# Two norms in one pass ahead of a convolution, its modulation later, and a feed-forward that begins with one token tile

## The chip, the cores and the metric

The kernel runs on one core of one Trainium2 chip. The metric is the time of one execution in microseconds on the device: the median of 3 runs is 2066.24 us (2065.29 to 2067.12). The engines are named as in the profile: PE is TensorE (matmuls; PEld are its weight loads), DVE is VectorE, ACT is ScalarE, POOL is GpSimd, SP is SyncE.

## What is computed

Two models run one after the other on 256 tokens of width 1024. The first is an attention layer with a large expert layer behind it. The second has two layers over the 256 tokens of its input ("latent") and 256 tokens of context; each layer is a mixer (first a short convolution, then a latent attention) and a feed-forward, and each of these begins with a norm whose output is scaled and shifted ("modulated") by rows computed from a conditioning vector `c`. What the change touches, cut from the reference:

```python
x = first_block(...)                  # ends with: return rmsnorm(h, final_norm_g)
silu_c = silu(c)
for i in range(2):
    sh1, sc1, g1, sh2, sc2, g2 = split(silu_c @ mod_w[i] + mod_b[i], 6)      # also from c_ctx, for the context
    a_lat = modulate(rms_norm(h_lat, norm_mix_g[i]), sh1, sc1)               # h * (1 + scale) + shift
    o_lat = short_conv_mixer(a_lat, ...) if i == 0 else mla_mixer(a_lat, ...)
    h_lat = h_lat + g1 * o_lat
    h_lat = h_lat + g2 * swiglu(modulate(rms_norm(h_lat, norm_ffn_g[i]), sh2, sc2), ...)
return h_lat
```

So the end of the first model is a norm over each token's 1024 values with the gain `final_norm_g`, and the beginning of the second is another norm over the result.

## The kernel before

**Matmuls.** Each product of two f32 matrices is made of three matmuls in a rounded f32 form: high part of the weight by high part of the activation, high by low, low by high. In `s_mode` these are lines 278 (`whi` by the high half of `act`), 279 (`whi` by the low half) and 280 (`wlo` by the high half). A piece of 128x128 of the weight is the stationary operand, and is loaded anew for each matmul; the activations stream past it, 512 columns where latent and context go together, 256 where only the 256 latent tokens do. In `m_mode` (lines 312, 313, 315) the weights stream.

**Weights.** `Stream W` loads weight tiles of 128x1024 in the order of a plan: SP issues the DMA into one of 4 `raw` buffers, ACT rounds it into `whi` (line 108), DVE subtracts to get `wlo` (line 109); there are 3 pairs of `whi` and `wlo`. A tile has a number in its name (`wlo474`). `W.prime(n)` brings the splits forward.

**Norm and modulation of an activation.** `norm_rows` squares and sums a token tile of 128x1024 on ACT, makes the mean on DVE (line 415, 128x1), raises it to -1/2 on POOL (`pow`, line 416) and multiplies on DVE. At the end of the first model it writes `hk = hk*yns*gate` (line 428, `gate` being the gain `fg`, which a POOL DMA of line 1161 spreads over the partitions); then `modulated` calls it again for the second norm (`yn`, line 426). `modulated` transposes `yn` on PE (line 1129), scales and shifts on ACT (line 1134, into `trs`), and splits into the two halves of `act` on DVE (the cast of line 1136, the subtraction of line 1137).

**The start of a mixer or feed-forward** works in pieces: `s_mode` takes `lead=(slices, function)`; its first three weight tiles go over the columns of the first slice, then the function makes the activations of the second slice, and the same three tiles go over it. For the convolution `BOTH` is used: first the 256 context tokens, then the 256 latent ones. The second feed-forward, `ffn(1, (0,), ...)`, has latent tokens alone, so it has no `lead`: each of its weight tiles is 24 matmuls of 256 columns.

**The modulation rows of the convolution** are made beside its matmuls. `second(M)` is a generator of background work, advanced by `run(..., bg, 1.7)` at each weight tile: `modulation(0, b)` for b=1 and b=2. It loads pieces of `mod_w` (`mraw`) with POOL's DMAs (line 488), multiplies and sums most of them on DVE (lines 504 and 506, into `ms`), the rest on PE (line 524), folds the sums on PE (line 529), adds the bias on DVE (line 531, `mb`), sends the result to DRAM and back with POOL's DMAs (`moddr<-mb`, line 534, then `mr<-moddr`, line 535), and transposes what comes back on PE (line 540). The first feed-forward has the same generator in it for the next layer, with buffers that are called `mem` there.

**Order.** Outside `tc.manual_schedule` blocks a scheduler orders the instructions of each engine by its own estimates; inside them, and for instructions with `tc.keep_in_program_order`, the order of the code holds. Each engine then works strictly in its order.

Of the kernel before, what the change touches and what calls it, by code (L numbers as in the profile page):

```python
# [19 lines left out]
P = 128  # L20
D = 1024
# [135 lines left out]
def tile_kernel(ctx: ExitStack, tc: tile.TileContext, I, out, cst, dbg=None):  # L157
# [320 lines left out]
    def modulation(i, b, raw, ahead, acc, room, sel, cc=None):  # L478
# [16 lines left out]
        loads = [load(n) for n in range(ahead)]  # L495
        sums = [acc(w) for w in ws]
        for n in range(2 * own):
            k, h = divmod(n, 2)
            r = loads.pop(0)
            hs = slice(h * D, (h + 1) * D)  # L500
            for w in ws:
                o, c = sums[w][:, hs], silu_c[:, w, k:k + 1]
                if k == 0:
                    V.tensor_scalar(o, r, c, None, op0=ALU.mult)
                else:
                    V.scalar_tensor_tensor(o, r, c, o, op0=ALU.mult, op1=ALU.add)  # L506
            if n + ahead < 2 * KC:
                loads.append(load(n + ahead))
            yield
# [255 lines left out]
    with ExitStack() as pp:  # L765
# [353 lines left out]

        def modulated(i, s, w, act, N_, xn=None, trs=2):  # L1120

            ah, al = act
            xn = xn or normed(w, N_)
            cs = slice(w * T, (w + 1) * T)
            for k0 in range(0, KC, 2):
                ps = misc()
                for k in range(2):
                    for t in range(2):
                        TE.transpose(ps[:, k * T + t * P:k * T + (t + 1) * P],
                                     xn[t][:, (k0 + k) * P:(k0 + k + 1) * P], ident)  # L1130
                a = N_.tile([P, 2, T], F32, tag="trs", name=uid("trs"), bufs=trs)
                for k in range(2):
                    o = w * 48 + 24 * s + k0 + k
                    S.activation(a[:, k, :], ps[:, k * T:(k + 1) * T], AF.Identity,
                                 scale=scl[i][:, 2 * w + s, k0 + k:k0 + k + 1], bias=modc[i][:, o:o + 1])
                V.tensor_copy(ah[:, k0:k0 + 2, cs], a)  # L1136
                V.tensor_tensor(al[:, k0:k0 + 2, cs], a, ah[:, k0:k0 + 2, cs].bitcast(F32), op=ALU.subtract)  # L1137

# [29 lines left out]
    for t in range(2):  # L1168
        for h in range(2):
            hs = slice(h * 512, (h + 1) * 512)  # L1170
            V.tensor_tensor(hx[t][:, hs], hx[t][:, hs], ov[t][h], op=ALU.add)
        norm_rows(BP, hx[t], "yn", fg, into=hx[t])
        dump(f"x1_{t}", hx[t])

# [12 lines left out]
    def ffn(i, ws, then, xn):  # L1187
# [6 lines left out]
        else:  # L1194
            modulated(i, 1, ws[0], act, BP, xn)
        ah, al = (x[:, :, :N] for x in act)
# [56 lines left out]
    with tc.tile_pool(name="conv", bufs=1) as C, tc.tile_pool(name="mod", bufs=1) as M:  # L1253
        bg = second(M)
        bt = res.tile([P, 2, KC, 2 * T], F32R, tag="x1", name="bt")
        bh, bl = bt[:, 0], bt[:, 1]
# [23 lines left out]
        for f in range(2):  # L1280
            run(s_mode(8, 512, ah, al, 2 * T, e_c,
                       lead=None if f else (BOTH, lambda: modulated(0, 0, 0, act, BP))), bg, 1.7)
            run(s_mode(8, 512, ah, al, 2 * T, lambda n, ps: e_u(n, ps, f)), bg, 1.7)
            run(s_mode(8, 512, ah, al, 2 * T, lambda n, ps: e_b(n, ps, f)), bg, 1.7)
        drain(bg)
# [37 lines left out]
    with ExitStack() as pm:  # L1323
# [208 lines left out]
        with tc.manual_schedule(engines={V.engine, S.engine, G.engine}):  # L1532
            run(m_mode(8, 1024, oh, ol, (0, 1), e_out))
            xn.append(finish(1))

    ffn(1, (0,), lambda t, h: nc.sync.dma_start(out[t * P:(t + 1) * P, h:h + 512], hx[t][:, h:h + 512]), xn)


# [25 lines left out]
```

## Time and profile before

| | before |
|---|---|
| median of 3 runs | 2066.24 us |
| profiled execution, its time | 2068.81 us |
| its span | 2067.0 us |
| PE busy | 2001.2 us, 97% |
| DVE busy | 1436.4 us, 69% |
| ACT busy | 904.7 us, 44% |
| POOL busy | 429.7 us, 21% |

The span is that of the instructions of one execution; its time has 1.8 us more around it. PE is busy for nearly the whole span, so time is won by taking away one of PE's few waits or some of its matmuls, and lost by adding to either. Rows of the timeline give the start, the duration, the engine, the line, the output and inputs, the shape, how many instructions a row gathers, and in brackets the idle time of the engine ahead of it with what ended it.

### The profile page before, as it was taken

The page shows a single profiled execution, that of the slowest core. Times are in us where ns is not written, and L with a number is a line of the kernel's source. Part 1 is how long each engine was busy: PE and PEld are TensorE (multiplying, and loading weights), DVE is VectorE, ACT ScalarE, POOL GpSimd, SP SyncE. Part 2 cuts the span into 40 slices and gives each one's busy share as a digit, 9 for nine tenths or more (in the row PEclk, how much of TensorE's full clock was granted, in tenths as well). Part 3 has the DMA queues.
Part 4 walks back from the last instruction along what each step waited for, and adds up shares of the span by engine and source line. Part 5 has one row for each costly group of instructions (what it writes and reads, how often), then busy time and mean ns, then how long its engine had stood idle before and what let it go on. Part 6 is the DMA issues. An engine that isn't in the chain of part 4 may idle for free.

```text
span 2067.0 us, 33205 instructions
## 1 busy us (share of the span) xinstructions
PE 2001.2 (97%) x12513; PEld 1743.1 (84%) x12513; DVE 1436.4 (69%) x2664; ACT 904.7 (44%) x1537; POOL 429.7 (21%) x394
## 2 busy tenths in 40 slices
PE   8999999999999999999999998999999989899999
PEld 7899899999999888888778777877888878568997
DVE  4666699978888888889577758656432477756554
ACT  4565544443444444445453223322322367555443
POOL 0002556655555100010021212021000034200000
PEclk9999999999999999999999999999999999999999
DMA  7445666665555544487565745466422345125654
GB/s 223 138 122 185 173 182 177 185 169 146 161 154 154 194 155 161 155 283 259 188 223 180 262 131 189 142 217 228 139 92 92 125 141 158 42 71 153 184 184 143
DMA packets 187172, 344.15 MB, mean 166 GB/s; under 512 B 18412, under 2 KB 95876, under 8 KB 187012
## 3 DMA queue, kind: packets, MB, share of 16 engines
q1 hardware_dynamic: 166036, 279.62, 43.9%
q0 software_dynamic: 17440, 59.14, 8.9%
q10 hardware_dynamic: 3536, 3.28, 0.6%
q8 instruction: 98, 1.61, 0.3%
q14 instruction: 62, 0.51, 0.1%
HBM read 339.78 MB, written 2.18 MB: 165 GB/s over the span
## 4 chain that ended last, share of the span: by engine, by line
PE 84%; issue 6%; DVE 5%; DMA 3%; ACT 1%; POOL 1%; POOLq 0%; DVEq 0%; ACTq 0%
PE acc L278 9%; PE acc L279 9%; PE acc L280 9%; PE acc L247 6%; PE acc L248 6%; PE acc L249 6%; PE acc L1070 5%; PE acc L1071 5%; PE acc L1074 5%; PE acc L312 5%; PE acc L313 5%; PE acc L315 5%; PE misc L1043 3%; DMA mem<-in_mod_w_dram 1%; PE misc L1468 1%
## 5 line engine op out<-in xcount | busy, mean ns | idle before, releaser
L109 DVE TENSOR_TENSOR wlo<-raw,whi 128x1024 fp32r<-128x1024 f32 (+2 forms) x401 | 484.0, 1210 | 399.9 <-ACT whi L108 398.7
L108 ACT ACTIVATE whi<-raw 128x1024 fp32r<-128x1024 f32 (+1 forms) x412 | 430.0, 1046 | 667.9 <-PE acc L279 271.4
L278 PE MATMUL acc<-act,whi 128*128 128x512 f32 (+1 forms) x944 | 323.1, 344 | 2.0 <-DVE act L1136 2.0
L280 PE MATMUL acc<-act,wlo 128*128 128x512 f32 (+1 forms) x944 | 322.1, 342 | 2.5 <-DVE wlo L109 2.5
L279 PE MATMUL acc<-act,whi 128*128 128x512 f32 (+1 forms) x944 | 322.9, 342 | 1.7 <-DVE act L1137 1.7
L247 PE MATMUL acc<-x2h,uhi 128*128 128x256 f32 x1024 | 293.7, 287 | 0.0
L248 PE MATMUL acc<-x2l,uhi 128*128 128x256 f32 x1024 | 290.6, 284 | 0.0
L249 PE MATMUL acc<-x2h,ulo 128*128 128x256 f32 x1024 | 290.6, 284 | 0.0
L791 POOL TENSOR_TENSOR ulo<-ut,uhi 128x768 fp32r<-128x768 f32 x128 | 238.0, 1861 | 173.8 <-ACT uhi L789 138.9
L789 ACT ACTIVATE uhi<-ut 128x768 fp32r<-128x768 f32 x128 | 108.6, 848 | 222.8 <-PE acc L248 90.8
L278 PEld LDWEIGHTS acc<-act,whi 128*128 128x128 f32 x944 | 180.9, 193 | 29.1 <-ACT whi L108 3.4
L1070 PE MATMUL acc<-whi,g 128*128 128x512 f32 x512 | 202.7, 396 | 0.2 <-ACT g L108 0.2
L280 PEld LDWEIGHTS acc<-act,wlo 128*128 128x128 f32 x944 | 181.3, 192 | 22.7 <-DVE wlo L109 2.9
L1071 PE MATMUL acc<-wlo,g 128*128 128x512 f32 x512 | 199.9, 390 | 0.3 <-DVE wlo L109 0.3
L279 PEld LDWEIGHTS acc<-act,whi 128*128 128x128 f32 x944 | 181.5, 192 | 21.9 <-DVE act L1137 2.5
L247 PEld LDWEIGHTS acc<-x2h,uhi 128*128 128x128 f32 x1024 | 197.9, 193 | 0.0
L248 PEld LDWEIGHTS acc<-x2l,uhi 128*128 128x128 f32 x1024 | 197.4, 193 | 0.0
L249 PEld LDWEIGHTS acc<-x2h,ulo 128*128 128x128 f32 x1024 | 197.3, 193 | 0.0
L1074 PE MATMUL acc<-whi,g 128*128 128x512 f32 x512 | 158.0, 390 | 0.0
L777 DVE STREAM_TRANSPOSE ut<-raw 128x768 f32<-128x768 f32 x128 | 123.4, 964 | 0.0
L506 DVE SCALAR_TENSOR_TENSOR mem<-mem,silu_c 128x1024 f32<-128x1024 f32 x84 | 106.7, 1284 | 17.2 <-DMA mem<-in_mod_w_dram 16.9
L1074 PEld LDWEIGHTS acc<-whi,g 128*128 128x128 f32 x512 | 96.0, 188 | 21.0 <-DVE g L109 0.5
(396 smaller groups left out, 3708.8 us busy)
## 6 DMA issues: line engine op xcount, KB each, us to landing
raw<-in_peer_u_dram SPq DMA_DIRECT2D x512, 128.0 KB, 3.2
raw<-in_peer_v_dram SPq DMA_DIRECT2D x128, 512.0 KB, 3.4
mem<-in_mod_w_dram POOLq DMA_DIRECT2D x64, 512.0 KB, 5.1
raw<-in_ffn_w_down_dram SPq DMA_DIRECT2D x50, 512.0 KB, 3.3
raw<-in_ffn_w_gate_dram SPq DMA_DIRECT2D x44, 512.0 KB, 3.8
raw<-in_ffn_w_up_dram SPq DMA_DIRECT2D x44, 512.0 KB, 3.7
raw<-in_w_in_dram SPq DMA_DIRECT2D x40, 512.0 KB, 3.9
mraw<-in_mod_w_dram POOLq DMA_DIRECT2D x32, 512.0 KB, 5.0
```

The source lines that it names most:

```text
L108: a = self.nc.scalar.activation(hi, src, AF.Copy)
L109: b = (eng or self.nc.vector).tensor_tensor(lo, src, hi.bitcast(F32), op=ALU.subtract)
L247: mm(ps, lh, rh, start=first, stop=False)
L248: mm(ps, lh, rl, start=False, stop=False)
L249: mm(ps, ll, rh, start=False, stop=last)
L278: mm(ps[n][:, cs], hi[:, k - k0, c], xh[:, k, cs], start=first, stop=False)
L279: mm(ps[n][:, cs], hi[:, k - k0, c], xl[:, k, cs], start=False, stop=False)
L280: mm(ps[n][:, cs], lo[:, k - k0, c], xh[:, k, cs], start=False, stop=last)
L791: a = eng.tensor_tensor(lo[:, c], x, hi[:, c].bitcast(F32), op=ALU.subtract)
L1070: mm(ov[t][h], gh[:, ts], vh[:, 0, hs], start=j == 0, stop=False)
L1071: mm(ov[t][h], gh[:, ts], vl[:, 0, hs], start=False, stop=False)
L1074: mm(ov[t][h], gl[:, ts], vh[:, 0, hs], start=False, stop=j == P - 1)
```

## The change

It has three parts. First, the two norms at the border of the models are made in one pass: ACT squares `hk`, DVE multiplies `hk` by the gain at once (without waiting for the first mean), ACT squares the product, and the two factors are combined in 128x1 columns of `cols`, so that `yn` is one multiplication of the product by the combined factor. `scaled()` multiplies `hk` by its own factor later. Second, the background generator of the convolution stops after its loads are issued, runs no step during the first `s_mode`, and then goes on at 1.95 steps a weight tile. Third, the second feed-forward begins with one token tile of 128 columns, then the other, and two of its weight tiles are split ahead of its norm's activations.

```diff
@@ modulation
         loads = [load(n) for n in range(ahead)]
         sums = [acc(w) for w in ws]
+        if cc is not None and b == 1:
+            yield
         for n in range(2 * own):
...
                 if k == 0:
-                    V.tensor_scalar(o, r, c, None, op0=ALU.mult)
+                    a = V.tensor_scalar(o, r, c, None, op0=ALU.mult)
+                    if cc is not None and b == 1:
+                        tc.keep_in_program_order(a)
@@ modulated
-        def modulated(i, s, w, act, N_, xn=None, trs=2):
+        def modulated(i, s, w, act, N_, xn=None, trs=2, one=None):
...
-            cs = slice(w * T, (w + 1) * T)
-            for k0 in range(0, KC, 2):
+            tiles = range(2) if one is None else [one]
+            n = P * len(tiles)
+            per = 2 * T // n
+            cs = slice(w * T + tiles[0] * P, w * T + tiles[0] * P + n)
+            for k0 in range(0, KC, per):
...
@@ end of the first model
-        norm_rows(BP, hx[t], "yn", fg, into=hx[t])
-        dump(f"x1_{t}", hx[t])
+    two = [cols[:, 3 * t:3 * t + 3] for t in range(2)]
+    for t in range(2):
+        y, s = BP.tile([P, D], F32, tag="yn", name=uid("yn"), bufs=2), two[t]
+        S.activation(y, hx[t], AF.Square, accum_out=s[:, 0:1])
+        V.tensor_tensor(hx[t], hx[t], fg, op=ALU.mult)
+        inv_rms(s[:, 0:1], D, BP)
+        S.activation(y, hx[t], AF.Square, accum_out=s[:, 1:2])
+        V.scalar_tensor_tensor(s[:, 1:2], s[:, 1:2], s[:, 0:1], s[:, 0:1], op0=ALU.mult, op1=ALU.mult)
+        inv_rms(s[:, 1:2], D, BP)
+        V.tensor_tensor(s[:, 2:3], s[:, 0:1], s[:, 1:2], op=ALU.mult)
+        V.tensor_scalar(y, hx[t], s[:, 2:3], None, op0=ALU.mult)
+        xn_first.append(y)
+
+    def scaled():
+        for t in range(2):
+            V.tensor_scalar(hx[t], hx[t], two[t][:, 0:1], None, op0=ALU.mult)
@@ ffn
         else:
-            modulated(i, 1, ws[0], act, BP, xn)
+            modulated(i, 1, ws[0], act, BP, xn, one=0)
+            lead = ([slice(0, P), slice(P, T)], lambda: modulated(i, 1, ws[0], act, BP, xn, one=1))
@@ convolution
         bg = second(M)
+        next(bg)
...
             run(s_mode(8, 512, ah, al, 2 * T, e_c,
-                       lead=None if f else (BOTH, lambda: modulated(0, 0, 0, act, BP))), bg, 1.7)
-            run(s_mode(8, 512, ah, al, 2 * T, lambda n, ps: e_u(n, ps, f)), bg, 1.7)
-            run(s_mode(8, 512, ah, al, 2 * T, lambda n, ps: e_b(n, ps, f)), bg, 1.7)
+                       lead=None if f else (BOTH, lambda: modulated(0, 0, 0, act, BP, xn_first))), bg if f else None, 1.95)
+            if not f:
+                scaled()
+            run(s_mode(8, 512, ah, al, 2 * T, lambda n, ps: e_u(n, ps, f)), bg, 1.95)
+            run(s_mode(8, 512, ah, al, 2 * T, lambda n, ps: e_b(n, ps, f)), bg, 1.95)
@@ end of the latent attention
             run(m_mode(8, 1024, oh, ol, (0, 1), e_out))
+            W.prime(1)
             xn.append(finish(1))
+            W.prime(3)
```

How the instructions move is seen in the lists of two engines at three places. Rows are an engine's instructions in order, with line, operation, output and inputs (names with their buffers' numbers), shape, and the engines or DMA queues that are waited for. Lines of the changed kernel have other numbers: 1171 becomes 1178, 1129 becomes 1136, 1136 and 1137 become 1143 and 1144, 524, 529 and 540 become 528, 533 and 544.

**First place: DVE at the beginning of the convolution.** Before, from the norm with the gain to the first cast of the latent activations; `ms` are the modulation's sums:

```order
L428 SCALAR_TENSOR_TENSOR hk0_9321<-hk0_9321,yns454_12978,gate452_12973 128x1024 [waits DMASW7_49,Pool_49]
L428 SCALAR_TENSOR_TENSOR hk0_9321<-hk0_9321,yns456_12986,gate452_12973 128x1024 [waits Pool_49]
L504 TENSOR_SCALAR ms479_13234<-mraw475_13227,silu_c_70 128x1024
L415 TENSOR_SCALAR yns463_13094<-yns463_13094 128x1 [waits Activation_49]
L506 SCALAR_TENSOR_TENSOR ms478_13233<-mraw476_13229,silu_c_70,ms478_13233 128x1024 [waits DMASW5_49]
L415 TENSOR_SCALAR yns465_13100<-yns465_13100 128x1 [waits Activation_49]
L506 SCALAR_TENSOR_TENSOR ms479_13234<-mraw476_13229,silu_c_70,ms479_13234 128x1024 [waits DVE_49]
L426 TENSOR_SCALAR yn462_13093<-hk0_9321,yns463_13094 128x1024 [waits Pool_49]
L426 TENSOR_SCALAR yn464_13099<-hk0_9321,yns465_13100 128x1024 [waits Pool_49]
L506 SCALAR_TENSOR_TENSOR ms478_13233<-mraw477_13231,silu_c_70,ms478_13233 128x1024 [waits DMASW6_49]
L506 SCALAR_TENSOR_TENSOR ms479_13234<-mraw477_13231,silu_c_70,ms479_13234 128x1024 [waits DVE_49]
L1136 CAST act437_11504<-trs467_13110 128x2x256 [waits Activation_49]
```

The same stretch in the changed kernel, from the multiplication of the second token tile by the gain:

```order
L1186 TENSOR_TENSOR hk0_9321<-hk0_9321,gate452_12973 128x1024 [waits DVE_49]
L1189 SCALAR_TENSOR_TENSOR cols_69<-cols_69 128x1 [waits Activation_49,Pool_49]
L415 TENSOR_SCALAR cols_69<-cols_69 128x1 [waits DVE_49]
L1191 TENSOR_TENSOR cols_69<-cols_69 128x1 [waits Pool_49]
L1192 TENSOR_SCALAR yn453_12979<-hk0_9321,cols_69 128x1024 [waits DVE_49]
L1189 SCALAR_TENSOR_TENSOR cols_69<-cols_69 128x1 [waits Activation_49]
L1197 TENSOR_SCALAR hk0_9321<-hk0_9321,cols_69 128x1024 [waits DVE_49]
L415 TENSOR_SCALAR cols_69<-cols_69 128x1 [waits DVE_49]
L1191 TENSOR_TENSOR cols_69<-cols_69 128x1 [waits Pool_49]
L1192 TENSOR_SCALAR yn454_12990<-hk0_9321,cols_69 128x1024 [waits DVE_49]
L1197 TENSOR_SCALAR hk0_9321<-hk0_9321,cols_69 128x1024 [waits DVE_49]
L1143 CAST act437_11504<-trs467_13126 128x2x256 [waits Activation_49]
```

All rows of `ms` have left this stretch, and the one that stood ahead of `wlo328`, at the very beginning of the convolution, has left too; the multiplications by `hk`'s own factor (L1197), meant for later in the code, stand ahead of the second `yn` and of the first cast.

**Second place: PE later in the convolution,** where the sums of the modulation b=1 are folded. Before, at the border of the weight tiles 337 and 338:

```order
L280 MATMUL acc505_13468<-act437_11504,wlo337_13414 128x512
L524 MATMUL misc508_13504<-mraw509_13505,cc_13217 32x512 [waits DMASW4_49]
L524 MATMUL misc508_13504<-mraw509_13505,cc_13217 32x512
L524 MATMUL misc508_13504<-mraw510_13507,cc_13217 32x512 [waits DMASW5_49]
L524 MATMUL misc508_13504<-mraw510_13507,cc_13217 32x512
L529 MATMUL misc508_13504<-ms478_13233,sel_13221 32x512 x4
L529 MATMUL misc508_13504<-ms479_13234,sel_13221 32x512 x4
L278 MATMUL acc502_13465<-act437_11504,whi338_13471 128x512 [waits Activation_49]
```

In the changed kernel the same group stands within the weight tile 339:

```order
L528 MATMUL misc502_13534<-mraw503_13535,cc_13008 32x512 [waits DMASW4_49]
L528 MATMUL misc502_13534<-mraw503_13535,cc_13008 32x512
L280 MATMUL acc494_13457<-act437_11504,wlo339_13502 128x512 [waits DVE_49]
L278 MATMUL acc495_13458<-act437_11504,whi339_13501 128x512
L279 MATMUL acc495_13458<-act437_11504,whi339_13501 128x512
L528 MATMUL misc502_13534<-mraw504_13537,cc_13008 32x512 [waits DMASW5_49]
L528 MATMUL misc502_13534<-mraw504_13537,cc_13008 32x512
L533 MATMUL misc502_13534<-ms460_13024,sel_13012 32x512 x4
L533 MATMUL misc502_13534<-ms461_13025,sel_13012 32x512 x4
L280 MATMUL acc495_13458<-act437_11504,wlo339_13502 128x512
```

The transposition of what comes back (L540 before, L544 in the changed kernel) stands at the end of weight tile 339 in both. From the last fold to it there are 48 matmuls of 512 columns before (the tiles 338 and 339), and 19 in the changed kernel. At the last modulation of the first feed-forward the same count goes from 48 to 31.

**Third place: DVE at the beginning of the second feed-forward.** Before, from the second `yn`:

```order
L447 TENSOR_SCALAR yn983_19084<-hk0_9321,nss457_12991 128x1024 [waits Pool_49]
L1136 CAST act984_19090<-trs986_19096 128x2x256 [waits Activation_49]
L1137 TENSOR_TENSOR act984_19090<-trs986_19096,act984_19090 128x2x256 [waits DVE_49]
L1136 CAST act984_19090<-trs988_19106 128x2x256 [waits Activation_49]
L1137 TENSOR_TENSOR act984_19090<-trs988_19106,act984_19090 128x2x256 [waits DVE_49]
```

In the changed kernel:

```order
L447 TENSOR_SCALAR yn977_19084<-hk0_9321,nss455_13001 128x1024 [waits Pool_49]
L109 TENSOR_TENSOR wlo475_19087<-raw475_19032,whi475_19086 128x1024 [waits DMAHW7_49,Activation_49]
L109 TENSOR_TENSOR wlo476_19091<-raw476_19038,whi476_19090 128x1024 [waits DMAHW0_49,Activation_49]
L1143 CAST act978_19098<-trs980_19104 128x4x128 [waits Activation_49]
L1144 TENSOR_TENSOR act978_19098<-trs980_19104,act978_19098 128x4x128 [waits DVE_49]
L1143 CAST act978_19098<-trs982_19116 128x4x128 [waits Activation_49]
```

Before, `wlo475` and `wlo476` stand behind the four casts and subtractions; now they stand ahead of the first cast, as `whi475` and `whi476` stand ahead of the first `trs` on ACT. A cast covers four pieces of one token tile instead of two pieces of both.

**PE at the same place,** in the changed kernel, from the last eight transpositions and matmuls of the first token tile to the second token tile's beginning:

```order
L278 MATMUL acc985_19130<-act978_19098,whi476_19090 128x128
L279 MATMUL acc985_19130<-act978_19098,whi476_19090 128x128
L280 MATMUL acc985_19130<-act978_19098,wlo476_19091 128x128
L1136 MATMUL misc986_19209<-ct_66,yn977_19084 128x128
L1136 MATMUL misc988_19221<-ct_66,yn977_19084 128x128 x4
L278 MATMUL acc984_19129<-act978_19098,whi474_19034 128x128 [waits DVE_49]
L278 MATMUL acc985_19130<-act978_19098,whi474_19034 128x128
```

Before, the 72 matmuls of the weight tiles 474 to 476 have 256 columns each and follow one another; now there are 72 of 128 columns, the last five transpositions of the second token tile, and 72 more of 128 columns, each with its own load of weights.

## Rows read from the trace of the kernel before

**Rows 1.** The page's part 1: busy time, share, instructions of each engine.

```profile
PE 2001.2 (97%) x12513; PEld 1743.1 (84%) x12513; DVE 1436.4 (69%) x2664; ACT 904.7 (44%) x1537; POOL 429.7 (21%) x394
```

**Rows 2.** Timeline of PE at the beginning of the convolution.

```profile
1073.48 0.39 PE L280 MATMUL acc<-act,wlo 128*128 128x256 f32 x1 [1.89 <-DVE wlo L109]
...
1085.27 3.56 PE L1129 MATMUL misc<-ct,yn 128*128 128x128 f32 x16 [3.15 <-DVE yn L426]
...
1090.04 0.39 PE L279 MATMUL acc<-act,whi 128*128 128x256 f32 x1 [0.28 <-DVE act L1137]
```

**Rows 3.** Timeline of DVE there.

```profile
1072.21 2.35 DVE L109 TENSOR_TENSOR wlo<-raw,whi 128x1024 fp32r<-128x1024 f32 x2
...
1084.38 1.57 DVE L426 TENSOR_SCALAR yn<-hk,yns 128x1024 f32<-128x1024 f32 x2
...
1088.26 0.42 DVE L1136 CAST act<-trs 128x512 fp32r<-128x512 f32 x1
```

**Rows 4.** Timelines of ACT and POOL there; the landing of L1161's DMA after its issue.

```profile
1081.38 1.06 ACT L422 ACTIVATE yn<-hk 128x1024 f32<-128x1024 f32 x1 [0.60 <-DVE hk L428]
...
1086.94 1.93 ACT L1134 ACTIVATE trs<-misc,modc,scl 128x256 f32<-128x256 f32 x4 [4.41 <-PE misc L1129]
...
1071.66 0.76 POOL L1161 DMA_DIRECT2D gate<-in_final_norm_g_dram  x1 [3.36 <-PE acc L1074]
1075.31 0.57 POOL L416 TENSOR_TENSOR yns<-yns,mhalf 128x1 f32<-128x1 f32 x1 [2.90 <-DVE yns L415]
...
DMA to landing us min/median/max: 5.7/5.7/5.7
```

**Rows 5.** Timelines of PE and POOL in the convolution; the landing of `mr`.

```profile
1141.17 2.30 PE L529 MATMUL misc<-ms,sel 128*32 128x512 f32 x14
...
1154.51 0.24 PE L540 MATMUL misc<-ct,mr 32*128 32x32 f32 x1
...
1145.28 1.17 POOL L534 DMA_DIRECT2D moddr<-mb  x2 [2.68 <-DVE sel L492]
...
1149.38 1.00 POOL L535 DMA_DIRECT2D mr<-moddr  x2 [2.38 <-DMA moddr<-mb]
...
DMA to landing us min/median/max: 1.7/1.7/2.0
```

**Rows 6.** Timeline of PE in the first feed-forward, second modulation.

```profile
1417.64 1.06 PE L529 MATMUL misc<-mem,sel 128*32 128x512 f32 x8
...
1428.39 0.25 PE L540 MATMUL misc<-ct,mem 16*128 16x16 f32 x1 [4.01 <-DMA mem<-moddr]
```

**Rows 7.** Timeline of PE there, last modulation.

```profile
1480.34 1.06 PE L529 MATMUL misc<-mem,sel 128*32 128x512 f32 x8
...
1492.45 0.23 PE L540 MATMUL misc<-ct,mem 16*128 16x16 f32 x1
```

**Rows 8.** Timelines of PE, DVE and ACT at the beginning of the second feed-forward.

```profile
1872.72 0.80 PE L278 MATMUL acc<-act,whi 128*128 128x256 f32 x2
...
1877.97 0.39 PE L280 MATMUL acc<-act,wlo 128*128 128x256 f32 x1 [0.63 <-DVE wlo L109]
...
1883.22 0.28 PE L280 MATMUL acc<-act,wlo 128*128 128x256 f32 x1
...
1869.43 0.75 DVE L447 TENSOR_SCALAR yn<-hk,nss 128x1024 f32<-128x1024 f32 x1 [0.67 <-POOL nss L416]
...
1872.70 0.69 DVE L1137 TENSOR_TENSOR act<-trs,act 128x512 fp32r<-128x512 f32 x1
...
1871.18 1.93 ACT L1134 ACTIVATE trs<-misc,modc,scl 128x256 f32<-128x256 f32 x4 [2.81 <-PE misc L1129]
```

**Rows 9.** Weight loads by form (busy us, mean ns), and a timeline row of PE.

```profile
L279 PEld LDWEIGHTS acc<-act,whi 128*128 128x128 f32 x944 | 181.5, 192 | 21.9 <-DVE act L1137 2.5
L529 PEld LDWEIGHTS misc<-ms,sel 128*32 128x32 f32 x32 | 1.1, 109 | 2.2 <-issue 2.2
...
228.43 2.06 PE L861 MATMUL misc<-room,qh 128*128 128x128 f32 x16
```

More of the change, by code (lines that the diff above doesn't have):

```diff
@@ L1118, in normed @@
             return [norm_rows(N_, hx[2 * w + t], "yn") for t in range(2)]
-        def modulated(i, s, w, act, N_, xn=None, trs=2):
+        def modulated(i, s, w, act, N_, xn=None, trs=2, one=None):
             ah, al = act
             xn = xn or normed(w, N_)
-            cs = slice(w * T, (w + 1) * T)
-            for k0 in range(0, KC, 2):
+            tiles = range(2) if one is None else [one]
[3 more added lines that the diff above has]
+            for k0 in range(0, KC, per):
                 ps = misc()
-                for k in range(2):
-                    for t in range(2):
-                        TE.transpose(ps[:, k * T + t * P:k * T + (t + 1) * P],
+                for k in range(per):
+                    for j, t in enumerate(tiles):
+                        TE.transpose(ps[:, k * n + j * P:k * n + (j + 1) * P],
                                      xn[t][:, (k0 + k) * P:(k0 + k + 1) * P], ident)
-                a = N_.tile([P, 2, T], F32, tag="trs", name=uid("trs"), bufs=trs)
-                for k in range(2):
+                a = N_.tile([P, per, n], F32, tag="trs", name=uid("trs"), bufs=trs)
+                for k in range(per):
                     o = w * 48 + 24 * s + k0 + k
-                    S.activation(a[:, k, :], ps[:, k * T:(k + 1) * T], AF.Identity,
+                    S.activation(a[:, k, :], ps[:, k * n:(k + 1) * n], AF.Identity,
                                  scale=scl[i][:, 2 * w + s, k0 + k:k0 + k + 1], bias=modc[i][:, o:o + 1])
-                V.tensor_copy(ah[:, k0:k0 + 2, cs], a)
-                V.tensor_tensor(al[:, k0:k0 + 2, cs], a, ah[:, k0:k0 + 2, cs].bitcast(F32), op=ALU.subtract)
+                V.tensor_copy(ah[:, k0:k0 + per, cs], a)
+                V.tensor_tensor(al[:, k0:k0 + per, cs], a, ah[:, k0:k0 + per, cs].bitcast(F32), op=ALU.subtract)
         with tc.tile_pool(name="cn", bufs=1) as N_:
@@ L1171, in tile_kernel @@
             V.tensor_tensor(hx[t][:, hs], hx[t][:, hs], ov[t][h], op=ALU.add)
-        norm_rows(BP, hx[t], "yn", fg, into=hx[t])
-        dump(f"x1_{t}", hx[t])
+    xn_first = []
+    two = [cols[:, 3 * t:3 * t + 3] for t in range(2)]
[13 more added lines that the diff above has]
+            V.tensor_scalar(hx[t], hx[t], two[t][:, 0:1], None, op0=ALU.mult)
+            dump(f"x1_{t}", hx[t])
     BOTH = [slice(T, 2 * T), slice(0, T)]
```

## Prediction

> **What bounds the kernel now.** The page's busy times come first: PE works for 97% of the span [rows 1], so the change can win only by shortening one of PE's waits, and loses by whatever it adds to PE. The list of PE's waits then shows where the few waits are, and the timelines of the engines around each of the two places that the change aims at show what ends last there.
>
> At the beginning of the convolution PE waits 1.89 us for `wlo`, then 3.15 us for the second norm's `yn`, then 0.28 us for the first subtraction [rows 2]. The first wait comes from DVE: the split of the two weight tiles ends at 1074.56 [rows 3], and a multiplication of the modulation stands ahead of it in DVE's order. The second is the norm's chain, which cannot begin its second half before the gain `fg` is there: POOL issues that DMA at 1071.66 and it lands 5.7 us later, at 1077.4 [rows 4]. The multiplications of the modulation stand between that chain's steps on DVE, and two of them ahead of the first cast: the first pair of `trs` is done about 1087.9 (half of 1.93 after 1086.94, [rows 4]), its cast begins at 1088.26 [rows 3].
>
> At the beginning of the second feed-forward PE's first matmul is at 1872.72, and what ends last before it is the second `yn`, from 1869.43 to 1870.18, then transpositions, then the activations from 1871.18 and a cast [rows 8]. Once started, it waits 0.63 us more for `wlo` and is through with the 72 matmuls of the first three weight tiles at 1883.34, one matmul spacing behind the start of the last one at 1883.22 [rows 8]. These run 0.12 us apart: 43 steps from 1877.97 to 1883.22 are 5.25 us.
>
> **Convolution, the norm.** The gain still lands at 1077.4. Then two multiplications by it at 1.2 us (like a `wlo`, 2.35 for two, [rows 3]) end at 1079.8; the squares, 1.06 us each [rows 4], run beside them and behind them to about 1081. Tile 0 goes on with small steps and a `pow` of 0.57 us [rows 4]; its `yn`, 0.8 us, ends about 1081.8. In the new order a multiplication of `hk` by its own factor, another 0.8 us, stands ahead of tile 1's `pow`, so tile 1's `yn` ends about 1084.5, where it now ends at 1085.95 [rows 3]. That is 1.4 us; a further 1.1 us comes from DVE's order, since cast and subtraction follow each other at once: 1086.94 - 1.4 + 0.97 for the first pair of `trs`, then 0.42 and 0.69 [rows 3, 8] give 1087.6 for the first L279 instead of 1090.04 [rows 2]. I take **-2.5 us**. The 1.89 us ahead of it goes too, but wins nothing: PE comes earlier to a wait that the gain's landing sets. Bounds: -1.2, if only the chain's own 1.4 less a few hand-overs is won; -4.4, if the 1.89 counts after all.
>
> **Convolution, the modulation that is put off.** Its twenty multiplications are the same, run on DVE beside matmuls, and cost nothing there by themselves. But the last fold on PE moves from 48 to 19 matmuls ahead of the transposition that needs its result. Now, from the fold's end at 1143.47, the bias, the DMA to DRAM from 1145.28 and the DMA back, issued from 1149.38 to 1150.38 and landing 1.7 us later, take until about 1152.1, 8.6 us; the transposition comes at 1154.51 [rows 5]. 48 matmuls fill these 11.04 us, so 19 fill 4.4 us, and PE would wait 4.2 us where now it does not wait. Some of the 8.6 is DVE's delay of the bias, so I take **+3.5 us**. Rows of the first feed-forward show such a wait: there 23 matmuls stand between, the result comes about 9.7 us behind the fold's end at 1418.70, and PE waits 4.01 us [rows 6]. Bounds: 0, if DMA and DVE are quick and matmuls are held up beforehand anyway; 5.2, with a chain of 9.7.
>
> **First feed-forward, last modulation.** By the order 48 matmuls become 31 there. 48 fill the 11.05 us from 1481.40 to 1492.45 without a wait [rows 7], so 31 fill 7.1; against chains of 8.6 [rows 5] to 9.7 [rows 6] that leaves 1.5 to 2.6 us. That modulation is of the latent tokens alone, with one DMA each way instead of two, so I take **+1.2 us**, and 0 and 2.6 as bounds.
>
> **Second feed-forward, one token tile.** The first matmul comes no earlier. The transpositions of tile 0 need not wait for the second `yn`, but DVE now makes `wlo475` and `wlo476` between that `yn` and the first cast: 1870.18 + 2.35 + 0.42 is 1872.95, against 1872.72. Then 144 matmuls of 128 columns replace 72 of 256. At the change of tiles the last five transpositions, four activations, a cast and a subtraction stand in a row, of which I put 0.8 us of transpositions and 1.8 us of waiting on the path (four activations at less than 1.93 for four of 256 columns, then 0.42 [rows 3, 8], part of it covered). The 72 matmuls now take 10.62 us where 0.12 apart would be 8.64; of the 1.98 over, 0.63 is the wait for `wlo`, which goes, and I keep 0.8 for the slow first matmuls (0.80 for two, [rows 8]). So the tiles are through at 1872.95 + 0.8 + 0.8 + 1.8 = 1876.35 plus 144 spacings.
>
> The spacing of a 128-column matmul in this form is not in the trace. Below it is 0.060, half of the 256 columns' 0.12. Above it is 0.119: L861's sixteen 128-column matmuls in plain f32 take 2.06 us, with a last one of 0.28 like that of 1883.22 [rows 8, 9]: 1.78 / 15. Between them decides the weight load, which every one of these matmuls has for itself: 192 ns for 128 columns, 109 for 32 [rows 9], so 0.865 ns a column, and 0.111 us for 128 if loads do not overlap each other. I take that, near L861: 16.0 us, through at 1892.35, **+9.0 us** against 1883.34. With 0.060 it is +1.65, with 0.119 +10.15. The Trainium skill ("TensorE: Matmul & The Clock Gate", "LDWEIGHTS") has the load grow with the weight's columns at P/1.2 ns, 107 ns for 128, which by itself would make +8.4; the slope in the rows agrees.
>
> **The sum.** -2.5 + 3.5 + 1.2 + 9.0 = +11.2 us. On the profiled execution's 2068.81 that is 2080.0; the median of the runs lies 2.57 lower, so **2077.4 us**. What this kernel's measurement can tell from no change is 0.2%, 4.1 us.
>
> **Rivals.** *Short matmuls are cheap.* If loads overlap and the spacing is 0.060, the last term is +1.65 and the sum +3.9: 2070.1. For it speaks that the streamed columns halve; against it the load's slope and L861. The same page of the Trainium skill ("Back-to-back issue gap") gives about 81 ns for a sustained stream at 128 columns, a halfway estimate of +4.7 for the term; no row here has such a stream. *The transposition does not wait.* With the fold's result back in time in both places, the sum is -2.5 + 9.0 = +6.5: 2072.7. For it: today's slack of 2.4 us at 1154.51 [rows 5]; against: rows 6. *Faster: DVE's order is what counts.* DVE stands behind every wait of rows 2. Freed of the modulation, it lets the norm's chain win the full 4.4 us, has the fold's bias ready at once so that its chain is hidden in both places, and has tile 1's cast ready at the change of tiles, which takes the 1.8 us away. That is -4.4 and 1874.55 plus 144 spacings against 1883.34, so the spacing decides: it is faster by more than 4.1 us below 0.063, and 0.060 gives -4.4 - 0.15 = -4.55: 2061.7. The DVE rows between 1084 and 1089 [rows 3] speak for it; the gain's landing at 1077.4 [rows 4] and the ACT and PE steps ahead of tile 1's cast speak against it.
>
> **How the numbers follow.** The forecast with a load-bound stream has 0.55, the rival without the transposition's wait 0.17, cheap short matmuls 0.17, the faster one 0.11. Bounds added up would be -2.75 to +16.8, with the covered change of tiles -4.55; the far ends together are unlikely. The range from 2065 to 2082.5 holds about 8 in 10. Of the cheap case half lies within 4.1 us, of the rest a little: slower 0.76, the same 0.15, faster 0.09.
>
> **What would show it.** Right: no wait for `wlo` at the start of the convolution, L279's first matmul of the latent half 2 to 3 us earlier against the end of the first model, a wait of 3 to 4 us at L544 for `mr` or its DMA, one of 1 to 2 us at the last modulation of the first feed-forward, and the 128-column L278 to L280 at 0.11 us, with a wait of about 1.8 us between the two token tiles. Wrong: matmuls of 128 columns at 0.06 to 0.08, no wait at L544, or a first matmul of the second feed-forward well before 1872.7 on this clock.

## The result: slower by 33 us, and the profile after

The changed kernel takes 2098.97 us (median of 4 runs, 2097.14 to 2101.18) against 2065.76 us (median of 4) for the kernel before: a ratio of 1.0167 (95% interval 1.0155 to 1.0180), 34 us slower by it. The direction was forecast, the size was not: 2077.4 us were predicted, and 2065.0 to 2082.5 as the range. The profiled execution took 2101.18 us, 32.4 more than that of before, with a span of 2099.3 us.

The page's busy times first, after the change:

```profile
PE 2027.2 (97%) x12585; PEld 1767.5 (84%) x12585; DVE 1439.4 (69%) x2670; ACT 906.2 (43%) x1545; POOL 426.8 (20%) x394
```

PE has 72 matmuls more, as the change says, and is busy 26 us longer than in [rows 1]: most of the loss isn't a wait, PE works longer. Where it does is seen in the stretches of 5 us at the beginning of the second feed-forward (columns: the stretch, its length, then busy us and instructions of PE, PEld, DVE, ACT and POOL, the granted clock as a share of 2.4 GHz, share of DMA, GB/s):

```profile
1875.00:1880.00 5.00, 2.46 (x11) 2.06 (x12) 4.26 (x8) 4.59 (x10) 0.56 (x1) 0.50 0.18 39
1880.00:1885.00 5.00, 5.00 (x26) 5.00 (x25) 1.08 (x3) 0.00 (x0) 0.00 (x0) 0.50 0.48 174
...
1890.00:1895.00 5.00, 5.00 (x26) 5.00 (x25) 0.00 (x0) 0.00 (x0) 0.00 (x0) 0.50 0.00 0
1895.00:1900.00 5.00, 3.71 (x17) 3.12 (x16) 2.24 (x4) 2.90 (x8) 0.00 (x0) 0.50 0.00 0
...
1915.00:1920.00 5.00, 5.00 (x31) 5.00 (x31) 0.95 (x1) 2.77 (x6) 0.00 (x0) 0.65 0.38 105
1920.00:1925.00 5.00, 5.00 (x44) 5.00 (x43) 2.45 (x2) 2.03 (x3) 0.00 (x0) 1.00 0.37 105
```

The granted clock falls to 0.50, the lower of its two levels (1.2 GHz), while PE waits for the norm, and stays there through both token tiles, although PE is then busy all the time but for the change of tiles. In the kernel before it falls at the same place, and is back at 1.00 before 1875 (the same stretches there):

```profile
1870.00:1875.00 5.00, 4.76 (x23) 4.49 (x24) 2.76 (x6) 3.39 (x7) 0.00 (x0) 0.56 0.00 0
1875.00:1880.00 5.00, 4.37 (x36) 4.13 (x36) 4.95 (x6) 3.43 (x5) 0.00 (x0) 1.00 0.16 35
```

The timeline of PE in the changed kernel shows what a matmul costs in it, and when the clock comes back:

```profile
1874.87 1.97 PE L1136 MATMUL misc<-ct,yn 128*128 128x128 f32 x8 [3.08 <-DVE yn L447]
1879.38 0.69 PE L278 MATMUL acc<-act,whi 128*128 128x128 f32 x2 [2.54 <-DVE act L1143]
...
1892.79 0.41 PE L278 MATMUL acc<-act,whi 128*128 128x128 f32 x1
1893.00 0.41 PE L279 MATMUL acc<-act,whi 128*128 128x128 f32 x1
...
1897.89 0.47 PE L278 MATMUL acc<-act,whi 128*128 128x128 f32 x1 [1.25 <-DVE act L1143]
...
1913.61 0.52 PE L278 MATMUL acc<-act,whi 128*128 128x256 f32 x1
1913.93 0.41 PE L279 MATMUL acc<-act,whi 128*128 128x256 f32 x1
...
1918.57 0.28 PE L280 MATMUL acc<-act,wlo 128*128 128x256 f32 x1
1918.69 0.28 PE L278 MATMUL acc<-act,whi 128*128 128x256 f32 x1
```

Matmuls of 128 columns are 0.213 us apart, and so are the first ones of 256 columns behind them; from 1918.57 on they run 0.12 us apart, and the granted clock is 1.00 in the stretch from 1920. In [rows 8] the three tiles' last matmul starts at 1883.22; with its 0.12 they are through 10.6 us after their first one at 1872.72. Now they take from 1879.38 to 1913.61, 34.2 us. That is 23.6 us of the loss, and the slow beginning of the fourth tile (23 matmuls from 1913.61 to 1918.57, 5.0 us instead of 2.8) another 2.2.

Of the rest, 6.7 us have come together before (the first matmul of this feed-forward is at 1879.38 instead of 1872.72). Up to the convolution the two executions differ by -1.8 us, which lies ahead of the change (the convolution's first matmul is at 1069.40, in the execution of before at 1071.20, two matmuls ahead of the wait of [rows 2]), so the convolution and what follows lose more than 8. The chain behind the modulation's last fold is read in the timelines of PE and POOL:

```profile
1146.93 2.30 PE L533 MATMUL misc<-ms,sel 128*32 128x512 f32 x14
...
1158.19 0.28 PE L544 MATMUL misc<-ct,mr 32*128 32x32 f32 x1 [4.41 <-DMA mr<-moddr]
...
1150.39 1.17 POOL L538 DMA_DIRECT2D moddr<-mb  x2 [2.03 <-DVE sel L492]
...
1155.76 0.99 POOL L539 DMA_DIRECT2D mr<-moddr  x2 [3.65 <-DMA moddr<-mb]
```

and the clock behind the wait in stretches of 4 us of PE alone (columns: the stretch, its length, then busy us and instructions, granted clock, share of DMA, GB/s):

```profile
1158.00:1162.00 4.00, 3.81 (x10) 0.50 0.68 230
1162.00:1166.00 4.00, 4.00 (x15) 0.73 0.98 359
1166.00:1170.00 4.00, 4.00 (x19) 1.00 0.86 333
```

PE waits 4.41 us where it waited for nothing in [rows 5], and then runs at half clock. Two rows of its timeline bound the slow stretch:

```profile
1158.40 0.80 PE L278 MATMUL acc<-act,whi 128*128 128x512 f32 x1
...
1164.37 0.40 PE L280 MATMUL acc<-act,wlo 128*128 128x512 f32 x1
```

The 14 matmuls between these two starts take 5.97 us; behind them they are 0.227 us apart, so this is about 2.8 us more. At the convolution's beginning the wait for `wlo` of [rows 2] is gone, but the sum of waits is not smaller (timelines of POOL, DVE and PE):

```profile
1069.87 0.53 POOL L1168 DMA_DIRECT2D gate<-in_final_norm_g_dram  x1 [3.37 <-PE acc L1078]
1076.88 2.36 DVE L1186 TENSOR_TENSOR hk<-hk,gate 128x1024 f32<-128x1024 f32 x2 [3.75 <-DMA gate<-in_final_norm_g_dram]
...
1081.64 0.63 PE L1136 MATMUL misc<-ct,yn 128*128 128x128 f32 x4 [3.45 <-DVE cols L1189]
1084.02 2.82 PE L1136 MATMUL misc<-ct,yn 128*128 128x128 f32 x12 [1.75 <-DVE yn L1192]
```

3.45 + 1.75 is 5.20, where [rows 2] have 1.89 + 3.15 + 0.28 = 5.32. DVE, free of the modulation, now stands still for 3.75 us until the gain has landed; its multiplication begins 7.0 us after the issue.

### The profile page after: what moved, and what is told of

Its sections match the earlier page's. It is cut to its first block, busy times and chain, and to the rows that moved or that the text cites. A ratio compares the mean times of both kernels' runs of the same rounds, so it can differ in the third digit from the quotient of the medians.

```text
span 2099.3 us, 33372 instructions
## 1 busy us (share of the span) xinstructions
PE 2027.2 (97%) x12585; PEld 1767.5 (84%) x12585; DVE 1439.4 (69%) x2670; ACT 906.2 (43%) x1545; POOL 426.8 (20%) x394
## 4 chain that ended last, share of the span: by engine, by line
PE 83%; issue 5%; DVE 5%; DMA 4%; ACT 1%; POOL 1%; POOLq 0%; DVEq 0%; ACTq 0%
PE acc L278 9%; PE acc L279 9%; PE acc L280 9%; PE acc L247 6%; PE acc L248 6%; PE acc L249 6%; PE acc L1074 5%; PE acc L1075 5%; PE acc L1078 5%; PE acc L312 5%; PE acc L313 5%; PE acc L315 5%; PE misc L1047 3%; DMA mem<-in_mod_w_dram 1%; DVE wlo L109 1%
## 5 line engine op out<-in xcount | busy, mean ns | idle before, releaser
L278 PE MATMUL acc<-act,whi 128*128 128x512 f32 (+2 forms) x968 | 337.8, 351 | 5.8 <-DVE act L1143 5.8
L279 PE MATMUL acc<-act,whi 128*128 128x512 f32 (+2 forms) x968 | 338.5, 350 | 1.5 <-DVE act L1144 1.5
L280 PE MATMUL acc<-act,wlo 128*128 128x512 f32 (+2 forms) x968 | 337.8, 349 | 0.0
L278 PEld LDWEIGHTS acc<-act,whi 128*128 128x128 f32 x968 | 193.5, 201 | 32.8 <-DVE act L1143 7.2
L279 PEld LDWEIGHTS acc<-act,whi 128*128 128x128 f32 x968 | 195.0, 201 | 23.2 <-DVE act L1144 2.1
L280 PEld LDWEIGHTS acc<-act,wlo 128*128 128x128 f32 x968 | 194.6, 201 | 21.5 <-issue 1.7
```

Source lines behind the costliest of these rows:

```text
L278: mm(ps[n][:, cs], hi[:, k - k0, c], xh[:, k, cs], start=first, stop=False)
L279: mm(ps[n][:, cs], hi[:, k - k0, c], xl[:, k, cs], start=False, stop=False)
L280: mm(ps[n][:, cs], lo[:, k - k0, c], xh[:, k, cs], start=False, stop=last)
```

## The experiments

Ratios are of the runs of a kernel to the runs of the kernel before on the same chip, with their 95% interval; 0.1% is 2.07 us.

**The first two parts, and the third.** `p1_only` is the changed kernel without its third part:

```diff
-            modulated(i, 1, ws[0], act, BP, xn, one=0)
-            lead = ([slice(0, P), slice(P, T)], lambda: modulated(i, 1, ws[0], act, BP, xn, one=1))
+            modulated(i, 1, ws[0], act, BP, xn)
...
-            W.prime(1)
             xn.append(finish(1))
-            W.prime(3)
```

Expected: 

> The change without its third part: two norms in one pass and the modulation put off, the second feed-forward as before. Theory: two thirds and more of the loss lie in the second feed-forward, so this one is slower than before by what the traces differ by ahead of it, 6 to 7 us (2072 to 2073), with a wait of some 4 us for mr at the transposition L544 and a granted clock near 0.5 for some us behind it. Rival: the 6 to 7 us there are a difference between two executions, and the first two parts change nothing: within 2 us of before.

Measured: 2071.67 us, 1.0032 (1.0019 to 1.0044), 6.6 us slower than before, as the first theory says. `p2_only` is the other part, the third alone.

Expected: 

> The third part alone: the second feed-forward with one token tile first, all else as before. Theory: the loss of that place is its own, whatever comes before: slower than before by 25 to 27 us (about 2092), with the granted clock at 0.50 from the first 128-column matmul to some us behind the last one, 0.213 us from one to the next. Rival: the clock was low because of what the first two parts left behind (DMA or engines late): then clearly less than 20 us, and the clock back at 1.00 within the stream.

Measured: 2089.13 us, 1.0115 (1.0100 to 1.0131), 23.8 us slower, a little under what was expected; its 128-column matmuls have the same mean durations as the changed kernel's, to 1 ns (417, 415 and 418 ns for L279, L280 and L278). The two together are 30 of the 34 us, and the intervals are wide enough for the rest. The third part costs by itself.

**Short matmuls on a clock that is up.** `short_hot` cuts one group of the kernel before into pieces, in the middle of the second feed-forward:

```diff
-                run(s_mode(8, gc, ah, al, N, e_up), bg, 1.75)
+                run(s_mode(8, gc, ah, al, N, e_up, cut=[slice(c, c + 128) for c in range(0, T, 128)] if i == 1 and g0 == 512 else None), bg, 1.75)
...
-        every_one = [slice(0, N)]
+        every_one = cut or [slice(0, N)]
```

Expected: 

> The kernel before, with one group of eight weight tiles in the middle of the second feed-forward (the second up projection group) done as 384 matmuls of 128 columns instead of 192 of 256; PE is busy at a granted clock of 1.00 before it. Theory A: a 128-column matmul is bound by its weight load, 0.107 to 0.115 us at full clock, and a stream of them keeps a clock that is up: clock 1.00, slower by 384 x 0.111 - 192 x 0.12 = 19.6 us. Theory B: the stream itself takes the clock down to 0.5: matmuls begin at 0.11 us and go to 0.213, slower by 45 to 59 us. Theory C: a 128-column matmul takes 0.213 us at any clock: slower by 59 us at a granted clock of 1.00. Cheap matmuls (0.060) would give no change.

The expectation counts the group twice: it has four weight tiles, 96 matmuls, which become 192. Measured: 2076.35 us, 1.0056 (1.0036 to 1.0075), 7 to 15 us slower. By theory A this is 192 x 0.111 - 96 x 0.12 = 9.8 us with that count. In the timeline of PE:

```profile
1905.28 0.22 PE L278 MATMUL acc<-act,whi 128*128 128x128 f32 x1
...
1926.56 0.28 PE L280 MATMUL acc<-act,wlo 128*128 128x128 f32 x1
1926.67 0.33 PE L278 MATMUL acc<-act,whi 128*128 128x256 f32 x1
```

and in one of the stretches of 5 us of PE alone, which are alike throughout the group:

```profile
1915.00:1920.00 5.00, 5.00 (x47) 1.00 0.36 97
```

192 matmuls take 21.39 us, 0.111 each, and the clock stays at 1.00. So neither does the stream take the clock down (theory B), nor does a matmul of 128 columns cost 0.213 us at any clock (theory C). A piece of 128 columns costs nearly as much as one of 256 at full clock (0.111 and 0.12 us) and the same at half clock (0.213 both): halving the columns about doubles PE's time. The weight loads slow with the clock too: 192 ns each in this group, 333 in the changed kernel's slow stream.

`short64_hot` is the same with pieces of 64 columns.

Expected: 

> As short_hot, in pieces of 64 columns: 384 matmuls in place of 96 of 256 (short_hot's group is 192 of 128 in place of 96; its expectation counted it twice). Theory: the weight load sets the spacing, so 64 columns take 0.111 us like 128: 42.7 us where 96 x 0.114 = 10.9 stand before, 32 us slower than before at a granted clock of 1.00; more, up to 71, if the clock falls, since less of the time is streaming. Rival: columns set the spacing with a floor near 0.06 us: 12 us slower, about as much as short_hot.

Measured: 2132.11 us, 1.0323 (1.0308 to 1.0338), 67 us slower. The timeline of PE:

```profile
1903.00 0.28 PE L279 MATMUL acc<-act,whi 128*128 128x64 f32 x1
1903.11 0.28 PE L280 MATMUL acc<-act,wlo 128*128 128x64 f32 x1
```

and its stretches of 5 us:

```profile
1900.00:1905.00 5.00, 5.00 (x46) 1.00 0.65 175
1905.00:1910.00 5.00, 5.00 (x43) 0.90 0.45 140
1910.00:1915.00 5.00, 5.00 (x25) 0.50 0.02 3
...
1980.00:1985.00 5.00, 5.00 (x29) 0.59 0.37 105
1985.00:1990.00 5.00, 5.00 (x44) 1.00 0.35 104
```

64 columns are 0.11 us apart like 128: what sets the spacing isn't the streamed columns. (The 0.114 of the expectation is 0.12 in the rows of 256 columns.) That it is the weight load fits the estimate of 0.111 us from [rows 9]; no run here changes the load itself. With pieces of 64 columns the clock does fall in the stream, with no wait ahead, and comes back only with the matmuls of 256 columns behind it.

**Keeping the clock up in the changed kernel.** `warm` adds matmuls of 512 columns into a bank that nobody reads, where PE would wait:

```diff
+            def keep_busy(n):
+                hi = W.parts[W.i][0]
+                ps = misc()
+                for _ in range(n):
+                    tc.keep_in_program_order(mm(ps, hi[:, 0, :P], hi[:, 0, :512], start=True, stop=True))
+
+            keep_busy(13)
             modulated(i, 1, ws[0], act, BP, xn, one=0)
+            keep_busy(15)
```

Expected: 

> The changed kernel, with 13 matmuls of 512 columns into an unused bank while PE would wait for the second feed-forward's yn, and 15 while it would wait for its first cast, so that PE isn't idle ahead of the 128-column stream. The output is that of the changed kernel. Theory A: the idle time lowered the clock and the stream only failed to bring it back: with the clock kept at 1.00 the stream runs at 0.107 to 0.115 us, 14 to 15 us less, and the 256-column matmuls behind it start fast, 2 us less: 16 us faster than the changed kernel, near 2083. Theory B: the stream takes the clock down itself, within a few us: no more than 4 us faster than the changed kernel. Theory C, a fixed 0.213 us: no change at all.

Measured: 2092.03 us, 1.0132 (1.0115 to 1.0148), some 7 us faster than the changed kernel: half of what theory A expects. The stretches of 4 us of all engines (columns as in the changed kernel's stretches of 5 us) show the other half:

```profile
1882.00:1886.00 4.00, 4.00 (x38) 4.00 (x38) 0.00 (x0) 0.02 (x1) 0.00 (x0) 1.00 0.00 0
1886.00:1890.00 4.00, 2.04 (x11) 1.66 (x10) 2.17 (x4) 2.89 (x8) 0.00 (x0) 0.80 0.02 4
1890.00:1894.00 4.00, 4.00 (x21) 4.00 (x20) 0.07 (x1) 0.50 (x1) 0.00 (x0) 0.50 0.00 0
```

and one row of PE's timeline what stands between:

```profile
1888.00 0.44 PE L278 MATMUL acc<-act,whi 128*128 128x128 f32 x2 [1.67 <-DVE act L1143]
```

The first token tile runs at full clock, 38 matmuls in 4 us; then PE waits 1.67 us for the second one's cast, the clock falls, and the second tile runs at half. `warm2` fills that wait too, with 12 matmuls behind the second tile's transpositions.

Expected: 

> As warm, with 12 more matmuls of 512 columns behind the second token tile's transpositions, where PE stood still for 1.67 and 0.29 us and the clock fell in the middle. Theory: an idle PE lowers the clock and short matmuls don't bring it back, but keep it; so with this wait filled the clock stays at 1.00 through both token tiles, the second 72 matmuls take 0.111 instead of 0.213 us (7.4 less) and the first 256-column tile behind them starts fast (2 less): 9 us faster than warm, near 2083. Rival: 72 short matmuls are as many as the clock bears; it falls in the second half anyway, and the time is that of warm.

Measured: 2080.98 us, 1.0071 (1.0056 to 1.0086), 12 us faster than `warm` and 19 to 20 faster than the changed kernel by the ratios. The same stretches:

```profile
1886.00:1890.00 4.00, 4.00 (x28) 3.53 (x26) 2.24 (x4) 2.33 (x7) 0.00 (x0) 1.00 0.02 4
1890.00:1894.00 4.00, 4.00 (x38) 4.00 (x38) 1.23 (x1) 1.29 (x2) 0.00 (x0) 1.00 0.00 0
```

The clock stays at 1.00 throughout, so the rival (72 short matmuls are as many as the clock bears) falls. Against `p1_only` the third part now costs 1.0071 - 1.0032, about 8 us, with the added matmuls in it. The short pieces alone account for 144 x 0.111 - 72 x 0.12 = 7.3 us.

`wide_primed` is the changed kernel with both token tiles at once again, and the two weight splits still ahead of them (the first hunk of `p1_only` alone).

Expected: 

> The changed kernel with the second feed-forward's activations and matmuls for both token tiles at once, 256 columns, as before, but with its two weight splits still ahead of them. Theory: it is the 128-column stream that costs; the splits ahead delay the first cast by about 2 us and take the 0.63 us wait for wlo away: within 3 us of p1_only, some 26 us faster than the changed kernel. Rival: the delay of the first cast by the splits lengthens PE's idle time and costs the clock: 5 us slower than p1_only or more.

Measured: 2070.83 us, 1.0027 (1.0016 to 1.0039), the same as `p1_only`. The splits ahead cost nothing that can be told; the matmuls of 128 columns are what costs. PE waits 3.05 and 0.78 us there and the clock falls to 0.50 as well, but with 256 columns it is at 1.00 again from 1878 on.

**The convolution.** `norms_only` is `p1_only` with the modulation at its old place and pace, `delay_only` is `p1_only` with the old norms.

Expected of `norms_only`: 

> The first part alone: two norms in one pass, the modulation at its old place and pace, the second feed-forward as before. Theory: the gain's landing bounds it, so it wins little, 0 to 3 us against before, and the fold stands 48 matmuls ahead of its transposition again, so there is no wait for mr. Rival: the norm's chain is itself slower on a DVE that it shares with the modulation: 1 to 3 us slower than before.

Expected of `delay_only`: 

> The second part alone: the modulation put off, norms and second feed-forward as before. Theory: the wait for mr and the half clock behind it are its price, and it frees DVE for the norm: 4 to 7 us slower than before. Rival: with the old norms the fold is ready earlier and there is no wait: no change.

Measured: `norms_only` 2068.55 us, 1.0017 (1.0008 to 1.0025), 3.5 us slower, near its rival's 1 to 3; `delay_only` 2071.01 us, 1.0022 (1.0012 to 1.0032), 4.5 us slower, with a wait of 3.8 us for `mr`. Neither part wins anything alone. In `norms_only` the wait for `wlo` is still there (1.86 us), and PE waits 4.82 and 0.91 us before the transpositions, where [rows 2] have 3.15 (PE and DVE):

```profile
1086.42 1.08 PE L1132 MATMUL misc<-ct,yn 128*128 128x128 f32 x4 [4.82 <-DVE yn L1188]
1088.42 2.82 PE L1132 MATMUL misc<-ct,yn 128*128 128x128 f32 x12 [0.91 <-DVE yn L1188]
...
1084.34 1.27 DVE L506 SCALAR_TENSOR_TENSOR ms<-mraw,silu_c,ms 128x1024 f32<-128x1024 f32 x1
1085.53 0.75 DVE L1188 TENSOR_SCALAR yn<-hk,cols 128x1024 f32<-128x1024 f32 x1
1086.43 1.28 DVE L506 SCALAR_TENSOR_TENSOR ms<-mraw,silu_c,ms 128x1024 f32<-128x1024 f32 x1
```

The new chain has more steps on DVE, and here a multiplication of the modulation of 1.27 us stands directly ahead of each `yn`.

`later_turn` is `p1_only` with the put-off result's transposition later:

```diff
         yield
         yield
+        if cc is not None and b == 1:
+            yield
+            yield
         n = 16 * len(ws)
```

Expected: 

> p1_only with the transposition of the put-off modulation's result two steps of the background later (43 matmuls behind the last fold instead of 19). Theory: the wait of 3.5 to 4.4 us for mr goes, and with it the stretch at half clock behind it, some 3 us: 6 to 8 us faster than p1_only, so 0 to 2 us faster than the kernel before. Rival: the wait only moves to the next thing that needs DVE or DMA there: no more than 3 us faster than p1_only.

Measured: 2066.39 us, 1.0007 (0.9998 to 1.0016); 5 us faster than `p1_only` by the ratios, no longer to be told from the kernel before, and without a wait at that transposition. So the wait with the half clock behind it was worth 5 us, and without it the two norms and the put-off modulation win nothing.

`early_gain` is `later_turn` with another buffer for the gain, `early_before` the kernel before with that buffer:

```diff
-    fg = gate_rows(I["final_norm_g"])
+    fg = res.tile([P, 8, D], F32, tag="x1", name="fg")[:, 0]
+    nc.gpsimd.dma_start(fg, I["final_norm_g"].partition_broadcast(P))
```

Expected of `early_gain`: 

> later_turn with the gain of the first norm loaded into a buffer that is free some 40 us earlier. Theory: at the convolution's start the landing of the gain alone sets when the norm's chain goes on, which is why two norms in one pass and a free DVE won nothing; with the gain there, the second yn is ready about when the context half's matmuls end, PE's waits of 3.5 and 1.7 us nearly go, and with them the half clock behind them: 5 to 8 us faster than later_turn, 4 to 8 us faster than the kernel before. Rival: the chain of ACT, DVE and POOL steps is as long without the landing: less than 2 us.

Expected of `early_before`: 

> The kernel before with that early gain and nothing else. Theory: the landing is only one of two things that hold the old chain; the modulation's multiplications and the order of its eight steps hold it as well, so half of the 5 us of waits goes: 2 to 4 us faster than before. Rival: as much as early_gain against before (then the two norms in one pass are worth nothing of themselves).

Measured: `early_gain` 2061.96 us, 0.9985 (0.9977 to 0.9994), 3 us faster than before and 4.5 faster than `later_turn` by the ratios, a little less than expected; `early_before` 2063.83 us, 0.9996 (0.9987 to 1.0005), no change that can be told. In its trace the wait for `yn` shrinks from 3.15 to 0.67 us, with 1.20 for the first cast behind it; but a multiplication of the modulation still stands ahead of `wlo`, and half a clock now follows that wait (timeline of PE, and one of its stretches of 2 us):

```profile
1072.94 0.39 PE L280 MATMUL acc<-act,wlo 128*128 128x256 f32 x1 [2.09 <-DVE wlo L109]
...
1074.00:1076.00 2.00, 2.00 (x11) 0.50 0.80 241
```

In `early_gain` the first multiplication by the gain follows its token tile at once, and PE's waits shrink (timelines of DVE and PE):

```profile
1072.76 1.22 DVE L1190 TENSOR_TENSOR hk<-hk,fg 128x1024 f32<-128x1024 f32 x1
...
1079.12 0.60 PE L1139 MATMUL misc<-ct,yn 128*128 128x128 f32 x4
1081.16 1.53 PE L1139 MATMUL misc<-ct,yn 128*128 128x128 f32 x12 [1.44 <-DVE yn L1196]
```

and the clock holds behind them (a stretch of 4 us of PE alone):

```profile
1084.00:1088.00 4.00, 4.00 (x34) 1.00 0.02 4
```

This version beats both kernels. Over `early_before` it is some 2 us ahead, and there the two intervals overlap: that the first two parts of the change are worth something once the gain is there and the transposition stands where its data are is likely, but only just told from noise.

## Why the prediction was wrong, point by point

**Second feed-forward, the step that failed.** The prediction took 144 spacings of 0.111 us, worked out from loads at full clock, and let only 0.8 us of "slow first matmuls" stand for the clock. The spacing at full clock was right to the digit: 21.39 us for 192 in `short_hot`, and about 8 us for the whole third part in `warm2` against the forecast +9.0. But the stream began at 0.50, because PE waits for 3.08 and 2.54 us ahead of it, and it never came back to 1.00: 0.213 instead of 0.111 for 144 matmuls is 14.7 us, and 2.2 behind them. Rows in hand spoke for half a clock at that place (in the kernel before, the first six matmuls from 1872.72 on are slow and the granted clock is 0.56 in the stretch from 1870); that it would end by itself as soon as before was taken for granted, when the matmuls that ended it before had twice the columns. `warm2` and `short_hot` show that the clock, and not the short matmul by itself, makes these 17 us.

The load's rule in the Trainium skill ("TensorE: Matmul & The Clock Gate", "LDWEIGHTS") agrees with 0.111 at full clock; at half clock the rows show 0.213, nearly twice that. The Trainium skill ("TensorE: Matmul & The Clock Gate", "Back-to-back issue gap"), named beside the rival of cheap short matmuls, has 81 ns for a sustained stream at 128 columns; these f32 streams measured 0.111, and even 64 columns 0.11, so that rival is out.

**The change of tiles** was put at 1.8 us and measured 1.25 us of waiting and five transpositions; the first matmul, forecast no earlier, came as far behind the last of the attention's as forecast, some 0.15 us later than before (forecast 0.23).

**The put-off modulation's wait** was forecast at 3.5 us and measured 4.41 (3.5 in `p1_only`, 3.8 in `delay_only`): the mechanism and its size hold. The half clock behind it, some 2.8 us, was left out. `later_turn` measures the two together as 5 us, against `p1_only`.

**The norm** was forecast to win 2.5 us and won nothing (`later_turn`). The landing was named as the limit but taken as 5.7 us from [rows 4]; the issue came 1.8 us earlier with the rest of that execution and the landing took 6.9 us, so the multiplication began at 1076.88, about when the landing was expected, while PE's first half had begun earlier and had no gap. What DVE gained was waited away. Its longer chain, and a longer stretch at half clock, took the rest: by stretches of 2 us some 7 us from 1083 on, where the kernel before has some 3.4 from 1086 on. `early_gain` shows that the landing held the new chain; `early_before` shows that it wasn't all that held the old one.

**First feed-forward, last modulation:** forecast +1.2, measured a wait of 0.34 us at L544 there. It stands 31 matmuls behind its fold as the order said, and the chain was shorter than that of [rows 6].

**The sum.** Forecast -2.5 + 3.5 + 1.2 + 9.0 = +11.2; measured by parts: first two parts +6.6 (`p1_only`), third part +23.8 (`p2_only`). By the trace, some 17 of the missing 22 us are the half clock in the second feed-forward, some 2.8 that in the convolution, and 2.5 the norm.

## What to carry to other kernels

Before matmuls are cut into shorter pieces to start sooner, look at what loads the stationary operand: where each had its own load, 128 columns cost PE here about what 256 do, and a start a few us earlier is paid with the double time of everything that is cut. Price a wait of PE with the stretch behind it, in rows at the clock that the trace grants there; and ask which matmuls come next, since a stream of short ones can stay at half clock for as long as it lasts. And when a chain is shortened, first find everything that it waits for: the shorter chain alone won nothing, the earlier landing alone won nothing that can be told, and both together won 3 us.

## What the hardware showed that was not expected

The granted clock depends on what came before, not on the stream alone. The same stream of 128-column matmuls held 1.00 for 21 us in `short_hot` and for both tiles in `warm2`, and stayed at 0.50 for both tiles in the changed kernel, 34 us, with PE busy but for one wait of 1.25 us; the first tile alone is 16 us without a wait. A wait of 1.67 us between two such streams was followed by a fall to 0.50 in `warm`; one of 1.44 us in `early_gain`, behind matmuls of 256 columns and four transpositions, was not. A stream of 64 columns fell from 1.00 to 0.50 with no wait ahead of it. After each of these falls the clock rose again only once matmuls of 256 columns ran. The rows show no reason beyond this, and none is claimed.
